# Two DeepNorm layers in split fp32: which sublayer makes which adaLN gate columns

## The chip, the cores and the metric

The kernel is one program on one core of a Trainium2 chip. The metric is the device time of one execution in microseconds. Engines are called PE (TensorE), PEld (its weight load), DVE (VectorE), ACT (ScalarE), POOL (GpSimd) and SP (SyncE, which here issues the large transfers).

## The reference

Two layers; each has three sublayers: an FFN (s = 0), a mixer (s = 1), an FFN (s = 2). Nine adaLN vectors per layer come from one condition vector `c`.

```
cond = silu(c)
for l in range(2):
    mod = (cond @ ada_w[l] + ada_b[l]).reshape(-1, 3, 3, 1024)   # [sublayer, (shift, scale, gate)]
    for s in range(3):
        u = x * (1 + mod[:, s, 1]) + mod[:, s, 0]
        h = mixer(u) if s == 1 else 0.5 * (silu(u @ w_g) * (u @ w_up)) @ w_out
        x = layer_norm(alpha * x + (1 + mod[:, s, 2]) * h, ln_g[l, s], ln_b[l, s])
```

`x` is 256 tokens by 1024, the FFN's hidden width 2816. The mixer is one projection of `u` for four kinds of attention and for four gates, four branch products, each times its sigmoid gate, summed, and an output product. Every number is fp32.

## The kernel before

**Weights.** Each weight tile of 128 x 1024 comes from HBM into a buffer `raw` (a pool of five, `RB`), with a transfer that SP issues (L256). ACT rounds it to `hi` (L259), DVE makes the rest `lo = raw - hi` (L264), and PE takes three passes of the exact parts (L283 to L285, or L287 to L289). `raw` is free once DVE has made `lo`; pairs `hi`, `lo` lie in pools of six. Loads are emitted with a priority (`HP`) that moves them ahead of other work.

**adaLN columns.** `ada_cols(l, s, v)` is a list of four steps. Each step loads two tiles of 128 x 1024 (L304, 512 KB, into the same five `raw` buffers and on the same queue of SP) and lets DVE reduce each against the condition vector (L305), which leaves one column of `shift`, `scale` or `gate`. A vector takes eight tiles. `ada_gate` transposes a finished gate, sends it through DRAM and spreads it over the rows (`G`).

**Who makes what.** `sub_steps(l, s, nxt)` gives every sublayer twelve steps: four for its own gate, eight for the shift and scale of the next sublayer; with some steps go the fetches of the LayerNorm's rows and `ada_gate` (before step 4). The last FFN has eight empty steps in place of a next sublayer. An FFN spreads its steps evenly over its 22 blocks (`hidden`, then `steps.pop`); the mixer runs one at every fourth tick from tick 6 on, a tick being half a pair of projection tiles or a quarter of a branch.

**Around them.** A block of an FFN ends in `post`: ACT's `th`, DVE's `th` (L525) and `h` (L527), which frees one of two PSUM banks `mm`, then `hh` and `hl`. The first two blocks after a boundary go through a transpose `hT` (L611) of an `h` (L609). A branch of the mixer is four products into two PSUM banks `tp`; DVE multiplies each with its gate (`tg`, L1063), which frees the bank. Before each boundary `next_mod` (L383 to L385), which has a high priority, needs the scale and shift of the next sublayer.

All engines run their own instructions in order. The order within an engine is set by the scheduler that builds the program, from the emission order and the priorities. The scheduler hands a freed `raw` buffer to the next transfer in SP's order.

Of the kernel before, what the change touches and what calls it, by code (L numbers as in the profile page):

```python
# [11 lines left out]
F32 = mybir.dt.float32  # L12
# [6 lines left out]
D = 1024  # L19
T = 256  # L20
# [13 lines left out]
# columns of mix_w_in  # L34
# [5 lines left out]
# pairs of 128-column tiles whose products come out transposed  # L40
# [7 lines left out]
# offsets in the constants  # L48
C_COS, C_SIN, C_END = 0, 256, 512
# offsets in the constants of sums  # L50
R_ONE, R_SUF, R_FOX = 0, 128, 256
R_END = 256 + 640
# offsets in the masks
C_MC, C_MT, C_MA = 0, 384, 768
M_END = 768 + 1152
# depths of buffers, priorities and places of the pieces of work among each other
# [51 lines left out]
def _consts():  # L108
    c = np.zeros((128, C_END), np.float32)
    i = np.arange(128)  # L110
    r = np.zeros((128, R_END), np.float32)
    r[:, R_ONE:R_ONE + 128] = 1.0
    r[:, R_SUF:R_SUF + 128] = (i[:, None] >= i[None, :])
    # minus sums of the first and of the second key tile, by columns (q0 k0, q1 k0, q1 k1)
    for o in (0, 128, 512):
        r[:, R_FOX + o:R_FOX + o + 128] = -(i[:, None] <= i[None, :]).astype(np.float32)
    r[:, R_FOX + 256:R_FOX + 384] = -1.0
    half = ROT // 2
    inv = np.float32(THETA) ** (-(np.arange(half, dtype=np.float32) * np.float32(2.0 / ROT)))
    ang = np.arange(T, dtype=np.float32)[:, None] * inv[None, :].astype(np.float32)  # L120
    cos, sin = np.cos(ang.astype(np.float64)).T, np.sin(ang.astype(np.float64)).T
    ct, st = np.ones((128, T)), np.zeros((128, T))
    for b in (0, 64):
        ct[b:b + 8], ct[b + 8:b + 16] = cos, cos
        st[b:b + 8], st[b + 8:b + 16] = sin, -sin
    c[:, C_COS:C_COS + 256], c[:, C_SIN:C_SIN + 256] = ct, st
    m = np.zeros((128, M_END), np.float32)
    q0, q1, k = i[:, None], i[:, None] + 128, np.arange(256)[None, :]
    bad = lambda ok: np.where(ok, 0.0, BIG)
    m[:, C_MC:C_MC + 128] = bad(k[:, :128] <= q0)  # L130
    m[:, C_MC + 128:C_MC + 384] = bad(k <= q1)
    m[:, C_MT:C_MT + 256] = -bad(i[:, None] < np.arange(256)[None, :])
    m[:, C_MT + 256:C_MT + 384] = -bad(i[:, None] < i[None, :])
    rules = [lambda d: (d >= 0) & (d <= 128), lambda d: (d >= 0) & (d % 4 == 0), lambda d: (d >= 0) & (d % 16 == 0)]
    for g, rule in enumerate(rules):
        m[:, C_MA + g * 128:C_MA + g * 128 + 128] = bad(rule(q0 - k[:, :128]))
        m[:, C_MA + 384 + g * 256:C_MA + 384 + g * 256 + 256] = bad(rule(q1 - k))
    return np.eye(128, dtype=np.float32), c, np.concatenate([m, r], axis=1).astype(ml_dtypes.bfloat16)
# [3 lines left out]
def trunk(ctx: ExitStack, tc: tile.TileContext, x, xT, crow, ada0, adac, adab, w_in0, w_in0x, gcol, bcol, ln_g, ln_b,  # L142
# [46 lines left out]
    # 2 silu(c) = c * (1 + tanh(c / 2))  # L189
# [43 lines left out]
    held = {"ins": [], "left": 0, "free": 0}  # L233

    def behind():
        """queue what follows behind the boundary that has just been emitted, on its engines."""
        stack = ExitStack()
        for i in held["ins"]:
            stack.enter_context(tc.issue_after(i))
        return stack  # L240
# [4 lines left out]
    def load(*srcs):  # L245
        """srcs: [128, n] each; the parts of their halves, which are loaded in turns."""
# [32 lines left out]
    def split_mm(ps, w, xh, xl, start, stop, w_stationary=True):  # L279
        """ps += w^T x by three passes of exact parts."""  # L280
# [11 lines left out]
    mods = {(l, s): {} for l in range(DEPTH) for s in range(3)}  # L292

    def ada_cols(l, s, v):
        """steps that leave sum_k cond_k W_kn + b_n (+ 1) in columns [128, n // 128]."""
        key = ("shift", "scale", "gate")[v]

        def run(c):
            if c == 0:
                mods[(l, s)][key] = ap_.tile([P, KT], F32, tag=key, bufs=2, name=key)  # L300
# [9 lines left out]
    def ada_gate(l, s):  # L310
        """steps that leave sum_k cond_k W_kn + b_n + 1 in every row of G."""
# [19 lines left out]
    def modulate(src, uh, ul, gd, bd, on_act):  # L331
        """parts of src * gd + bd; src may lie in PSUM."""
# [9 lines left out]
    def fetch_row(dst, row):  # L342
        """a row of DRAM into one partition of each 32; spread_row spreads it from there."""
# [16 lines left out]
    def sub_steps(l, s, nxt):  # L360
        """steps beside a sublayer's products: its gate and its LayerNorm's rows, the modulation of what follows."""
        st = mods[(l, s)]
        nx = ada_cols(*nxt, 0) + ada_cols(*nxt, 1) if nxt else [lambda: None for _ in range(8)]
# [11 lines left out]
        seq = ada_cols(l, s, 2) + nx  # L375
        return [both(*before.get(n, []), f) for n, f in enumerate(seq)]

# [10 lines left out]
    def boundary(rt, accs, i, G, g, b, u, nxt):  # L388
        """rows: r = ALPHA x + G O, then LayerNorm; into u: its modulation for what follows."""
# [78 lines left out]
        def finish(gate):  # L468
            """the second token tile, behind products of the first one in what follows."""
# [22 lines left out]
    # column groups of a sublayer's last products: (token tile, first column, columns)  # L492
    TAIL = ((0, 0, 512), (0, 512, 512), (1, 0, 512), (1, 512, 512))

# [1 line left out]
    def ffn(l, s, u, nxt, steps, first=False):  # L496
# [61 lines left out]
        if first:  # L558
            f0 = F0
            banks = [mm_bank() for _ in range(2)] + [acc_bank() for _ in range(4)] + [tp_bank() for _ in range(2)]  # L560
            for n in range(KT):
# [3 lines left out]
                for k in range(2 * F0):  # L565
                    # up to block N0 the last two banks hold the pair after the first F0
# [72 lines left out]
    def mixer(l, u, nxt, steps):  # L639
# [9 lines left out]
        # pieces of attention, which take their turns between those of the projections  # L649
# [51 lines left out]
        def vproj(srcs, width, piece, extra=0):  # L701
            """extra: leading columns, of wf and of the index keys."""
# [29 lines left out]
        # columns of V in pieces of 384: B 0, C 256, D 512, A 768  # L732
# [7 lines left out]
        def scores(pss, qs, ks, start=True):  # L740
            """of two heads in their halves of the rows: q-tile 0 by keys 0..127, q-tile 1 by keys 0..255."""
# [4 lines left out]
        def transposed(p0, p1):  # L746
            """[q, keys] blocks -> [keys, (k0 q0, k0 q1, k1 q1)]."""
# [8 lines left out]
        def pv(y, heads):  # L756
            """y[64 j.., :] = sum over (v of key tile 0, of key tile 1, transposed weights) of heads[j]."""
# [11 lines left out]
        def y_out(y, k, t=None):  # L769
            """parts of what a branch is fed with; t: of one token tile only."""  # L770
# [10 lines left out]
        def soft(s_out, parts):  # L781
            """softmax of negated scores; parts: per q-tile a list of (psum, mask, columns of s_out)."""
# [35 lines left out]
        def index_scores(h):  # L818
# [11 lines left out]
            if h == 3:  # L830
                # keys that may not be seen take the value that marks a taken key
# [36 lines left out]
        def a_scores(t):  # L868
            """q-tile t of both heads of the three groups."""
# [16 lines left out]
        def a_blocks(t):  # L886
            """(group, head, key tile), in the order in which their products are taken."""
# [37 lines left out]
        def c_logs():  # L925
            """the logarithms of C, and with them those of D's forget gates."""
# [14 lines left out]
        def c_sums(j):  # L941
            """of two heads: the sums, and with them the weights."""
# [34 lines left out]
        def plan():  # L977
            """what runs after which piece of the projections, in steps of half a pair."""
# [24 lines left out]
            for n in range(S0, S0 + 4 * len(steps), 4):  # L1003
                on(n, step)
# [20 lines left out]
        # gates and branch products  # L1025
# [92 lines left out]

    u = new_u()
    for l in range(DEPTH):  # L1120
        u = ffn(l, 0, u, (l, 1), sub_steps(l, 0, (l, 1)), first=l == 0)
        u = mixer(l, u, (l, 2), sub_steps(l, 1, (l, 2)))
        nxt = (l + 1, 0) if l + 1 < DEPTH else None
        u = ffn(l, 2, u, nxt, sub_steps(l, 2, nxt))
# [55 lines left out]
```

## Time and profile before

| | |
|---|---|
| time, median of 3 runs (lowest, highest) | 1333.25 us (1328.18, 1336.28) |
| profiled execution, first to last instruction | 1336.7 us |
| PE, PEld busy | 1279.5, 1185.8 us |
| DVE, ACT, POOL busy | 1045.9, 655.5, 193.0 us |
| TensorE clock granted, mean | 0.987 of 2.4 GHz |
| moved by DMA | 300.41 MB, mean 225 GB/s |

The runs' times and the profiled execution come from different executions; 1336.7 us is the profiled one's own time. A busy time is the union of the instructions of an engine. Matmuls overlap each other in it, so a small wait of PE doesn't show as idle. The boundaries between the six sublayers lie at about 207, 471, 671, 872 and 1134 us.

### The profile page before, as it was taken

What the parts mean: (1) busy time and instruction counts of PE and PEld (TensorE: products, weight loads), DVE (VectorE), ACT (ScalarE), POOL (GpSimd) and SP (SyncE); (2) the same over time, 40 slices, a digit from 0 to 9 for tenths busy, and PEclk for the clock granted to TensorE, in tenths of its full rate; (3) what the DMA queues carried; (4) which work ended last, traced back from release to release, by engine and by line L of the source; (5) the groups of instructions that cost most, each with busy time, mean ns of one, the idle gap of its engine ahead of it and who ended that gap; (6) DMA issues with size and microseconds to landing.
All of it is one profiled execution on the core that took longest, in us unless ns stands there. A gap on an engine that the chain in (4) does not pass through costs nothing.

```text
span 1336.7 us, 23420 instructions
## 1 busy us (share of the span) xinstructions
PE 1279.5 (96%) x9178; PEld 1185.8 (89%) x9178; DVE 1045.9 (78%) x1661; ACT 655.5 (49%) x1023; POOL 193.0 (14%) x190
## 2 busy tenths in 40 slices
PE   6999998999999999999989999989999999899997
PEld 6989987899989889998979998988999998899996
DVE  7787888999855898876698876698997658986565
ACT  4644355457754445534345434354567544454440
POOL 0130004305011040000040000052060110400000
PEclk9999999999999989999999999989999999999999
DMA  9888992767755539877439877437677554596540
GB/s 340 317 294 317 314 312 95 254 193 254 254 177 188 190 132 319 307 265 248 149 138 315 301 266 243 140 126 248 201 252 242 189 190 158 174 328 199 184 142 32
DMA packets 85846, 300.41 MB, mean 225 GB/s; under 512 B 10604, under 2 KB 12316, under 8 KB 85736
## 3 DMA queue, kind: packets, MB, share of 16 engines
q1 hardware_dynamic: 84392, 298.00, 65.7%
q8 instruction: 72, 1.18, 0.3%
q10 hardware_dynamic: 576, 0.60, 0.1%
q0 software_dynamic: 768, 0.32, 0.1%
q14 instruction: 38, 0.31, 0.1%
HBM read 297.81 MB, written 1.07 MB: 224 GB/s over the span
## 4 chain that ended last, share of the span: by engine, by line
PE 57%; DMA 17%; DVE 16%; issue 5%; ACT 4%; POOL 1%; SPq 0%; DVEq 0%; ACTq 0%; POOLq 0%
PE mm L283 12%; PE mm L284 11%; PE mm L285 11%; DMA raw<-in_w_in_dram 10%; DVE lo L264 6%; DMA raw<-in_adac_dram 6%; PE acc L289 5%; PE acc L287 5%; PE acc L288 5%; DVE raw L305 2%; ACT hi L259 2%; DVE rt L415 2%; PE tp L283 1%; PE tp L284 1%; PE tp L285 1%
## 5 line engine op out<-in xcount | busy, mean ns | idle before, releaser
L264 DVE TENSOR_TENSOR lo<-raw,hi 128x1024 fp32r<-128x1024 f32 (+2 forms) x421 | 509.6, 1223 | 178.9 <-ACT hi L259 176.1
L259 ACT CAST hi<-raw 128x1024 fp32r<-128x1024 f32 (+1 forms) x422 | 434.6, 1040 | 354.6 <-PE mm L284 133.9
L283 PE MATMUL mm<-uh,hi 128*128 128x256 f32 x2032 | 576.8, 284 | 6.4 <-DVE h L527 5.4
L284 PE MATMUL mm<-ul,hi 128*128 128x256 f32 x2032 | 573.2, 282 | 0.0
L285 PE MATMUL mm<-uh,lo 128*128 128x256 f32 x2032 | 572.5, 282 | 0.3 <-DVE lo L264 0.3
L283 PEld LDWEIGHTS mm<-uh,hi 128*128 128x128 f32 x2032 | 385.0, 190 | 13.9 <-issue 6.3
L284 PEld LDWEIGHTS mm<-ul,hi 128*128 128x128 f32 x2032 | 385.1, 190 | 1.4
L285 PEld LDWEIGHTS mm<-uh,lo 128*128 128x128 f32 x2032 | 385.0, 190 | 0.8 <-DVE lo L264 0.5
L305 DVE CUSTOM_DVE_ANT_0 raw<-raw,cond_row,adab 128x1024 f32<-128x1024 f32 x128 | 164.1, 1292 | 43.2 <-DMA raw<-in_adac_dram 43.0
L287 PE MATMUL acc<-hi,hh 128*128 128x512 f32 x352 | 140.6, 399 | 1.7 <-ACT hh L533 1.6
L288 PE MATMUL acc<-lo,hh 128*128 128x512 f32 x352 | 139.1, 395 | 0.0
L289 PE MATMUL acc<-hi,hl 128*128 128x512 f32 x352 | 138.3, 396 | 0.4 <-POOL hl L534 0.4
L289 PEld LDWEIGHTS acc<-hi,hl 128*128 128x128 f32 x352 | 66.0, 188 | 17.8 <-DVE hl L534 1.2
L533 ACT CAST hh<-h 128x256 fp32r<-128x256 f32 x82 | 33.2, 405 | 98.7 <-DVE h L527 96.9
L287 PEld LDWEIGHTS acc<-hi,hh 128*128 128x128 f32 x352 | 66.1, 188 | 17.0 <-ACT hh L533 3.3
L405 POOL TENSOR_TENSOR rstd<-rstd,nhalf 128x1 f32<-128x1 f32 x12 | 7.6, 633 | 494.7 <-DVE rstd L404 494.7
L288 PEld LDWEIGHTS acc<-lo,hh 128*128 128x128 f32 x352 | 66.1, 188 | 13.9
L1065 POOL TENSOR_TENSOR merged<-merged,tg 128x512 f32<-128x512 f32 x16 | 23.0, 1451 | 143.8 <-DVE tg L1063 97.1
L289 PE MATMUL acc<-hi,ul 128*128 128x256 f32 (+1 forms) x128 | 41.3, 323 | 2.2 <-DVE ul L434 2.2
L287 PE MATMUL acc<-hi,uh 128*128 128x256 f32 (+1 forms) x128 | 41.7, 326 | 0.0
L534 DVE TENSOR_TENSOR hl<-h,hh 128x256 fp32r<-128x256 f32 x74 | 31.1, 420 | 12.6 <-ACT hh L533 12.6
L288 PE MATMUL acc<-lo,uh 128*128 128x256 f32 (+1 forms) x128 | 40.5, 316 | 0.0
(242 smaller groups left out, 1583.8 us busy)
## 6 DMA issues: line engine op xcount, KB each, us to landing
raw<-in_w_in_dram SPq DMA_DIRECT2D x174, 512.0 KB, 5.6
raw<-in_adac_dram SPq DMA_DIRECT2D x128, 512.0 KB, 5.4
raw<-in_mpair_dram SPq DMA_DIRECT2D x104, 512.0 KB, 5.1
raw<-in_w_out_dram SPq DMA_DIRECT2D x88, 512.0 KB, 5.4
ada<-in_ada_dram SPq DMA_DIRECT2D x16, 512.0 KB, 6.7
raw<-in_mwo_dram SPq DMA_DIRECT2D x16, 512.0 KB, 4.1
raw<-in_mv_dram SPq DMA_DIRECT2D x16, 384.0 KB, 3.5
raw<-in_mbr_dram SPq DMA_DIRECT2D x12, 512.0 KB, 3.9
```

The source lines that it names most:

```text
L259: nc.scalar.copy(hi[:, :half], raw[:, :half])
L264: held["lo"] = nc.vector.tensor_sub(lo[:, :half], raw[:, :half], hi[:, :half].bitcast(F32)).ins
L283: nc.tensor.matmul(ps, lhsT=wh, rhs=xh, start=start, stop=False)
L284: nc.tensor.matmul(ps, lhsT=wh, rhs=xl, start=False, stop=False)
L285: nc.tensor.matmul(ps, lhsT=wl, rhs=xh, start=False, stop=stop)
L287: nc.tensor.matmul(ps, lhsT=xh, rhs=wh, start=start, stop=False)
L288: nc.tensor.matmul(ps, lhsT=xh, rhs=wl, start=False, stop=False)
L289: return nc.tensor.matmul(ps, lhsT=xl, rhs=wh, start=False, stop=stop).ins
L305: nc.vector.tensor_tensor_reduce(raw, raw, cond_row, 0.5, adab_sb[:, l * 3 + s, v, n:n + 1], ALU.mult, ALU.add, accum_out=t[:, n:n + 1])
L415: nc.vector.tensor_scalar(rt[:, t, hs], rt[:, t, hs], mv[t][:, 0:1], rstd[t], op0=ALU.subtract, op1=ALU.mult)
L533: nc.scalar.copy(hh, h)
L534: eng.tensor_sub(hl, h, hh.bitcast(F32))
```

## The change

The steps of each sublayer come from a plan, `ada_plan`. A mixer makes, after its own gate and the next FFN's shift and scale, that FFN's gate as well: 16 steps. The FFN behind the first mixer, (0,2), makes the shift and scale of the next layer's first FFN and half of that FFN's gate: 10 steps. That next FFN, (1,0), makes the other half and the shift and scale of its mixer: 10 steps. The last FFN, (1,2), makes none: its steps carry only the fetches, in 8 empty steps. The first FFN is as it was. In the mixer the first nine steps stand where they stood; the further ones come every 3 or 4 ticks in place of every 4. Gate columns get four buffers in place of two. Comments were taken out, which shifts line numbers by 10 to 12.

```diff
-                mods[(l, s)][key] = ap_.tile([P, KT], F32, tag=key, bufs=2, name=key)
+                mods[(l, s)][key] = ap_.tile([P, KT], F32, tag=key, bufs=4 if v == 2 else 2, name=key)
...
-    def sub_steps(l, s, nxt):
+    def ada_plan():
+
+        gate = {k: ada_cols(*k, 2) for k in mods}
+        mod = {k: ada_cols(*k, 0) + ada_cols(*k, 1) for k in mods}
+        work = {}
+        for l in range(DEPTH):
+            here, after, nxt = (l, 0), (l, 2), (l + 1, 0)
+            work[here] = (gate[here] if l == 0 else gate[here][2:]) + mod[(l, 1)]
+            work[(l, 1)] = gate[(l, 1)] + mod[after] + gate[after]
+            work[after] = mod[nxt] + gate[nxt][:2] if nxt in mods else []
+        return work
+
+    def sub_steps(l, s):
...
-        seq = ada_cols(l, s, 2) + nx
+        seq = list(ada[(l, s)])
+        seq += [lambda: None] * (GG + GD + 1 - len(seq))
...
-            for n in range(S0, S0 + 4 * len(steps), 4):
-                on(n, step)
+            for n in range(len(steps)):
+                on(S0 + 4 * min(n, 8) + 7 * max(0, n - 8) // 2, step)
...
+    ada = ada_plan()
```

The change moves instructions on DVE and SP. On DVE, in the second half of the (0,2) FFN, around the last two tiles of columns, before:

```order
L525 SCALAR_TENSOR_TENSOR th<-th,mm 128x256
L305 ISA raw,scale<-raw,cond_row,adab 128x1024
L305 ISA scale 128x1
L264 TENSOR_TENSOR lo<-raw,hi 128x1024
L383 TENSOR_TENSOR gd<-gcol,scale 128x8
L384 TENSOR_TENSOR bd<-bcol,scale 128x8
L527 SCALAR_TENSOR_TENSOR h<-th,mm 128x256
```

and after:

```order
L305 ISA raw,gate<-raw,cond_row,adab 128x1024
L305 ISA gate 128x1
L264 TENSOR_TENSOR lo<-raw,hi 128x1024
L537 SCALAR_TENSOR_TENSOR th<-th,mm 128x256
L539 SCALAR_TENSOR_TENSOR h<-th,mm 128x256
L264 TENSOR_TENSOR lo<-raw,hi 128x1024
L546 TENSOR_TENSOR hl<-h,hh 128x256
```

The last tile is a gate's, it stands ahead of `th`, and nothing stands between `th` and `h`.

On DVE, in the first mixer, ahead of the `tg` of the third branch (numbers tell buffers apart), before:

```order
L779 TENSOR_TENSOR y_4364<-acc_4552,y_4364 128x256
L264 TENSOR_TENSOR lo_4761<-raw_4758,hi_4760 128x1024
L264 TENSOR_TENSOR lo_4767<-raw_4764,hi_4766 128x1024
L264 TENSOR_TENSOR lo_4833<-raw_4830,hi_4832 128x1024
L264 TENSOR_TENSOR lo_4839<-raw_4836,hi_4838 128x1024
L264 TENSOR_TENSOR lo_4897<-raw_4894,hi_4896 128x1024
L264 TENSOR_TENSOR lo_4903<-raw_4900,hi_4902 128x1024
L1063 SCALAR_TENSOR_TENSOR tg_4559<-tg_4559,tp_4770 128x512
```

and after (the second half of it; ahead of it stand two more `lo` and the reduction of raw_4880):

```order
L305 ISA raw_4883,gate_4692<-raw_4883,cond_row_84,adab_89 128x1024
L305 ISA gate_4692 128x1
L264 TENSOR_TENSOR lo_4846<-raw_4843,hi_4845 128x1024
L264 TENSOR_TENSOR lo_4852<-raw_4849,hi_4851 128x1024
L305 ISA raw_4974,gate_4692<-raw_4974,cond_row_84,adab_89 128x1024
L305 ISA gate_4692 128x1
L305 ISA raw_4977,gate_4692<-raw_4977,cond_row_84,adab_89 128x1024
L305 ISA gate_4692 128x1
L264 TENSOR_TENSOR lo_4916<-raw_4913,hi_4915 128x1024
L264 TENSOR_TENSOR lo_4922<-raw_4919,hi_4921 128x1024
L1075 SCALAR_TENSOR_TENSOR tg_4565<-tg_4565,tp_4777 128x512
```

Four reductions of gate tiles now stand among the six `lo`, in two pairs, each pair with two `lo` behind it. SP's queue for the same place, after the change:

```order
L256 DMA raw_4771<-in_mbr_dram 128x1024
L304 DMA raw_4790<-in_adac_dram 128x1024
L304 DMA raw_4793<-in_adac_dram 128x1024
L256 DMA raw_4843<-in_mpair_dram 128x1024
L256 DMA raw_4849<-in_mpair_dram 128x1024
L304 DMA raw_4880<-in_adac_dram 128x1024
L304 DMA raw_4883<-in_adac_dram 128x1024
L256 DMA raw_4913<-in_mpair_dram 128x1024
L256 DMA raw_4919<-in_mpair_dram 128x1024
L304 DMA raw_4974<-in_adac_dram 128x1024
L304 DMA raw_4977<-in_adac_dram 128x1024
```

Before, no L304 stood between these projections' loads. DVE reads raw_4974 right after the two `lo` that follow its reading of raw_4883; SP can issue raw_4974 when raw_4883 has been read. The second mixer has the same order.

## Rows read from the trace of the kernel before

**Rows 1.** The page: span, busy time by engine, the column reductions and their transfers

```profile
span 1336.7 us, 23420 instructions
...
PE 1279.5 (96%) x9178; PEld 1185.8 (89%) x9178; DVE 1045.9 (78%) x1661; ACT 655.5 (49%) x1023; POOL 193.0 (14%) x190
...
L305 DVE CUSTOM_DVE_ANT_0 raw<-raw,cond_row,adab 128x1024 f32<-128x1024 f32 x128 | 164.1, 1292 | 43.2 <-DMA raw<-in_adac_dram 43.0
...
raw<-in_adac_dram SPq DMA_DIRECT2D x128, 512.0 KB, 5.4
```

**Rows 2.** Three stretches: PE, PEld, DVE, ACT, POOL busy (instructions), clock, DMA share, GB/s

```profile
495.40:670.20 174.80, 172.41 (x1184) 159.57 (x1185) 134.12 (x195) 79.74 (x112) 1.70 (x3) 0.99 0.75 257
695.30:871.20 175.90, 172.56 (x1184) 159.50 (x1185) 133.10 (x195) 78.40 (x112) 1.70 (x3) 0.99 0.74 252
1158.40:1328.00 169.60, 169.54 (x1176) 157.22 (x1176) 112.18 (x154) 72.75 (x99) 2.14 (x3) 1.00 0.57 191
```

**Rows 3.** PE's waits, 774 to 842 us; the first row also answers 574 to 641

```profile
PE mm L283 <- DVE h L527: 2.3, 1, 2.3
PE acc L287 <- ACT hh L533: 0.9, 1, 0.9
```

**Rows 4.** Slices of the mixers and the FFNs, columns as in rows 2

```profile
370.00:440.00 70.00, 67.83 (x559) 66.29 (x558) 39.39 (x50) 34.45 (x59) 11.90 (x8) 0.98 0.56 182
400.00:410.00 10.00, 10.00 (x87) 10.00 (x86) 4.34 (x4) 4.68 (x8) 0.00 (x0) 1.00 0.54 179
610.00:620.00 10.00, 8.60 (x54) 8.37 (x55) 7.21 (x13) 5.72 (x8) 0.00 (x0) 0.83 0.90 330
810.00:820.00 10.00, 7.66 (x51) 7.54 (x51) 7.92 (x15) 5.25 (x8) 0.00 (x0) 0.83 0.97 344
380.00:390.00 10.00, 7.83 (x55) 7.79 (x54) 8.01 (x19) 5.26 (x14) 5.95 (x4) 0.83 0.50 167
1040.00:1050.00 10.00, 8.70 (x73) 7.72 (x72) 7.70 (x21) 4.82 (x16) 3.17 (x3) 1.00 0.83 283
```

**Rows 5.** DVE's timeline in (0,2): start, duration, instruction [idle before, releaser]

```profile
604.62 1.28 DVE L305 CUSTOM_DVE_ANT_0 raw<-raw,cond_row,adab 128x1024 f32<-128x1024 f32 x1 [3.85 <-DMA raw<-in_adac_dram]
...
608.11 0.42 DVE L525 SCALAR_TENSOR_TENSOR th<-th,mm 128x256 f32<-128x256 f32 x1
608.44 1.28 DVE L305 CUSTOM_DVE_ANT_0 raw<-raw,cond_row,adab 128x1024 f32<-128x1024 f32 x1
...
610.93 0.42 DVE L527 SCALAR_TENSOR_TENSOR h<-th,mm 128x256 f32<-128x256 f32 x1
```

**Rows 6.** PE's waits, 370 to 440 us and 1035 to 1103 us

```profile
PE tp L283 <- DVE tg L1063: 2.2, 1, 2.2
...
PE tp L283 <- DVE tg L1063: 1.3, 1, 1.3
```

**Rows 7.** DVE's timeline in the first mixer, ahead of the second branch's `tg`

```profile
372.16 1.28 DVE L305 CUSTOM_DVE_ANT_0 raw<-raw,cond_row,adab 128x1024 f32<-128x1024 f32 x1 [4.71 <-DMA raw<-in_adac_dram]
...
373.38 2.35 DVE L264 TENSOR_TENSOR lo<-raw,hi 128x1024 fp32r<-128x1024 f32 x2
377.16 1.28 DVE L305 CUSTOM_DVE_ANT_0 raw<-raw,cond_row,adab 128x1024 f32<-128x1024 f32 x1 [1.43 <-DMA raw<-in_adac_dram]
...
381.48 0.68 DVE L1063 SCALAR_TENSOR_TENSOR tg<-tg,tp 128x512 f32<-128x512 f32 x1
```

**Rows 8.** SP's timeline: the issue of the tile that DVE reads at 377.16

```profile
373.48 0.33 SPq L304 DMA_DIRECT2D raw<-in_adac_dram  x1
```

**Rows 9.** DVE's timeline in the first mixer, around the third branch's `tg`

```profile
399.43 1.23 DVE L264 TENSOR_TENSOR lo<-raw,hi 128x1024 fp32r<-128x1024 f32 x1 [3.69 <-ACT hi L259]
...
413.35 1.45 DVE L1063 SCALAR_TENSOR_TENSOR tg<-tg,tp 128x512 f32<-128x512 f32 x2
415.83 0.69 DVE L1063 SCALAR_TENSOR_TENSOR tg<-tg,tp 128x512 f32<-128x512 f32 x1 [1.02 <-PE tp L285]
```

**Rows 10.** PE's waits, 1150 to 1180 us

```profile
PE hT L611 <- DVE h L609: 0.7, 1, 0.7
```

More of the change, by code (lines that the diff above doesn't have):

```diff
@@ L358, in both @@
         return run
-    def sub_steps(l, s, nxt):
+    def ada_plan():
[9 more added lines that the diff above has]
+    def sub_steps(l, s):
         st = mods[(l, s)]
-        nx = ada_cols(*nxt, 0) + ada_cols(*nxt, 1) if nxt else [lambda: None for _ in range(8)]
         def fetch(key, row):
@@ L1117, in first_block @@
         modulate(xT_sb[:, n], u[0][:, n], u[1][:, n], c0[:, n, 1:2], c0[:, n, 0:1], True)
+    ada = ada_plan()
     u = new_u()
     for l in range(DEPTH):
[L1121 to L1124, printed above, removed]
+        u = ffn(l, 0, u, (l, 1), sub_steps(l, 0), first=l == 0)
+        u = mixer(l, u, (l, 2), sub_steps(l, 1))
+        u = ffn(l, 2, u, (l + 1, 0) if l + 1 < DEPTH else None, sub_steps(l, 2))
 def _layout(x, c, ada_w, ada_b, ln_g, ln_b, ffn_w_in, ffn_w_out, mix_w_in, mix_b_gate, mix_b_forget, mix_w_branch, mix_w_out):
```

## The prediction

> **What bounds the kernel now.** I read the page first [rows 1]: TensorE (PE) is busy for 1279.5 of 1336.7 us. It is in nearly every stage the engine that the others serve, so a change that only moves VectorE (DVE) and DMA work can win no more than the places where PE stands still because of that work. A busy PE is counted with overlapping ends, so the second view is a comparison of equal work. In each of the last three FFNs I take the stretch from the hT transposes to the last product [rows 2]. The (0,2) and (1,0) FFNs run 1184 matmuls in 174.8 and 175.9 us; the (1,2) FFN runs the same ones, less eight boundary transposes, in 169.6 us. The first two make nearly all of their 24 column tiles in there, the last most of its 8. The 5.2 and 6.3 us are what the columns can cost an FFN.
>
> The third view, PE's waits, says where they are [rows 3]. Each of the two FFNs has one wait of 2.3 us of a first pass (L283) for `h` (L527), and (1,0) has 0.9 us more for `hh`. Right after, the granted clock of a 10 us slice is 0.83 [rows 4]: some of it ran at 1.2 GHz instead of 2.4, which lost (1 - 0.83) x 10 = 1.7 us. So 4.0 of 5.2 us and 4.9 of 6.3 us are named; the rest goes to the eight transposes and gaps too short to be listed.
>
> The fourth view, DVE's timeline, says why `h` was late [rows 5]. DVE works in order. It sat 3.85 us for a column tile, got to `th` at 608.11, and then did another L305 (608.44), a `lo` and the two small operations of `next_mod` before `h` at 610.93. The last scale column was pulled in between `th` and `h` because `next_mod` (high priority) needs it.
>
> In the mixers the same view shows one PE wait each, for `tg` (L1063) of 2.2 and 1.3 us [rows 6]; the first is followed by a clock of 0.83, the second by 1.00 [rows 4]. Here too DVE had waited for columns: 4.71 us, then 1.43 us, then `tg` at 381.48 [rows 7].
>
> **The change, part by part.** The number of column tiles stays 128, so DMA bytes and DVE work in total stay. The first FFN keeps its 12 steps. What moves is 4 tiles out of each middle FFN, 8 out of the last one, and 8 into each mixer.
>
> *Middle FFNs.* Each loses 4 transfers and 4 reductions of 1.29 us [rows 1], 5.2 us of DVE work that was hidden except at its end. There the order changes too: the scale columns come earlier, the last two steps are gate columns that no high-priority work asks for, and `h` follows `th` at once. Had `h` followed `th` at 608.44, it would have been done at 608.86, about when PE came for the bank. I therefore take back the whole named loss: 4.0 + 4.9 = 8.9 us. Bounds: 0 (DVE still waits for a gate tile just before a `th`, and the wait stays) and 5.2 + 6.3 = 11.5 us (all of it).
>
> *Last FFN.* Its first gate tile stood between `th` and `h` of the first block, and PE waited 0.7 us for that `h` [rows 10]. No tile is left there: -0.7 us (0 to -1.0). `ada_gate` finds its gate already made. The steps without work move the rows' fetches to later blocks, on GpSimd's queue, which idles there; still long before the boundary: 0.
>
> *Mixers.* Eight more transfers and reductions, all in the stretch with the gate projections: 8 x 1.29 = 10.3 us of DVE in 70 us of which it is busy for 39.4 [rows 4], so the work alone costs nothing. What costs is order. SP issues in order, into five raw buffers, which DVE frees in its order: a transfer starts when the fifth reading before it is done. If DVE reads a column tile soon after that, it stands still for the rest of the transfer, and everything behind it waits: `lo`, `y` and `tg`.
>
> There are two places. First, the `tg` of 381.48. Two scale reductions now come one pair of weight halves earlier, and one gate reduction that is issued only three readings before comes in front of `tg`. Walking the chain with the durations of the rows gives `tg` at about the same time; I take 0, with -2.2 - 1.7 (the wait and its clock fall go) and +2 for each mixer as bounds.
>
> Second, the four `tg` of the third branch, at 413.35 now [rows 9]. Before, only six `lo` (and `y`) stood ahead of them from 399.43 on. Afterwards the six `lo` have four gate reductions among them in two pairs. From 400.0 (one more reduction comes just before) the work is 6 x 1.17 + 4 x 1.22 = 11.9 us (two `lo` take 2.35 us, and the start after a reduction comes 1.22 later [rows 7]). Each pair is released by the reading two `lo` ahead of it, so DVE stands for Lat - 2.35 each time, Lat being the time from issue to landing, and, by estimate, 0.4 us more for the second tile of a pair. The first `tg` starts at 400.0 + 11.9 + 2 (Lat - 2.35) + 0.8 = 408.0 + 2 Lat. PE needs it at 413.7: its product for the third `tg` was ready at 415.83, is 12 matmuls long (1.4 us at 87 in 10 us [rows 4]), and needs the bank which the first `tg`, of 0.7 us, frees. So PE waits 2 Lat - 5.7 us. A transfer alone took from 373.48 to 377.16, 3.7 us [rows 7, 8]; the median of all column transfers is 5.4 us [rows 1], most of them in FFNs with the DMA busier. With two or three in flight I take 4.1, nearer to the lone one: 2.5 us. After waits of 2.2 and 2.3 us the clock fell, after 1.3 us it did not [rows 3, 4, 6]: I add 1.7. That is 4.2 us in each mixer, 8.4 us; with 3.7 us in place of 4.1, 1.7 us of wait; with 5.4, 5.1 us.
>
> The Trainium skill ("DMA: Bandwidth & Descriptors", Anatomy of one DMA) gives 2.0 us plus the bytes at 436 GB/s for one transfer on GpSimd's path, an estimate of 3.2 us for 512 KB. By that, the wait would be 0.7 us, without a fall of the clock, and the sum 7 us lower. The one lone transfer of this trace took longer (3.7 us), so the rows stand.
>
> **Sum**, against the profiled execution's 1336.7 us: -8.9 - 0.7 + 8.4 = -1.2, 1335.5 us. The runs' median is 1333.25, 3.4 us below the profiled one; from the median I forecast **1332 us**: no change. One per cent, 13 us, is about what a measurement of this kernel can tell from no change.
>
> **The rivals.**
> - *The mixers hide it all.* If transfers land in 3.7 us or less and PE's wait stays near the 1.3 us that left the clock alone, each mixer costs 0 to 1.7 us, and the FFNs' 9.6 us stay: 1324 to 1327, say 1325. For it: the DMA share is 0.56 there [rows 4]. Against: DVE waited 4.71 us for a tile in the same stage [rows 7].
> - *The mixers lose more than the FFNs win (slower).* The mechanism is the same queue of DVE in front of the third branch's `tg`. With Lat at 5.4 a mixer loses 5.1 + 1.7, and with the first `tg` late by another 1.0 it is 7.8: 1333.25 - 9.6 + 15.6 = 1339, up to 1346 if the FFNs give back only a third. It decides from 2 Lat - 5.7 + 1.7 = 4.8, that is Lat = 4.4 us, on.
> - *The FFNs don't get faster.* The tiles left at the end of a middle FFN are released only two readings ahead, as those of before were; DVE then still comes late to `th`. The gain is 0 to 2 us and the mixers' 8.4 remain: 1340.
>
> **How the numbers follow.** Forecast 0.5 (1328 to 1336), mixers hide it 0.27, mixers lose more 0.14, FFNs keep their waits 0.09. The range 1321 to 1343 holds the first, nearly all of the second (its end with 11.5 us from the FFNs is 1333.25 - 12.2 = 1321), and most of the other two. Faster by over 1% (below 1320) takes the FFNs' upper bound and a mixer gain together: 0.05. Slower by over 1% (above 1346.6) takes Lat above 5.4 and no gain in the FFNs: 0.06. The rest, 0.89, is within 1%.
>
> **What the profile after would show.** The stretches of rows 2 for the (0,2) and (1,0) FFNs at about 170.5 us, with no wait for `h` and a clock of 1.00 to their ends: the FFN term is right. A PE wait for `tg` of 2 to 3 us in each mixer, some 35 us after the first one, with DVE idle for column tiles before it: the mixer term is right; its absence makes the first rival, a wait of 5 us the second. The (1,2) FFN without a wait at hT. The prediction is wrong by more than its range if the eight tiles hold up `hi` and `lo` so long that PE waits for weights in the gate projections, which the trace of before shows nowhere.

## The result, and the profile after

The changed kernel takes 1357.58 us in the median of 5 runs (1350.64 to 1359.34), the kernel before 1333.25 (1328.18 to 1336.28): a ratio of 1.0168, interval 1.0141 to 1.0195. It is slower by 1.4 to 1.95%, and its time lies above the range of the prediction (1321 to 1343). The profiled execution after (1350.64 us) is the shortest of the five, and the one before, with a span of 1336.7 us, took longer than any of the timed ones (1336.28 us at most), so the two pages differ by only 12.0 us.

The page after, with the rows that answer to [rows 1] and the group of products that wait for `tg`:

```profile
span 1348.7 us, 23426 instructions
...
PE 1276.7 (95%) x9178; PEld 1182.0 (88%) x9178; DVE 1049.3 (78%) x1661; ACT 656.0 (49%) x1023; POOL 192.0 (14%) x190
...
L305 DVE CUSTOM_DVE_ANT_0 raw<-raw,cond_row,adab 128x1024 f32<-128x1024 f32 x128 | 166.5, 1310 | 54.3 <-DMA raw<-in_adac_dram 54.0
...
L283 PE MATMUL tp<-y,hi 128*128 128x256 f32 x112 | 37.0, 330 | 17.4 <-DVE tg L1075 17.4
...
raw<-in_adac_dram SPq DMA_DIRECT2D x128, 512.0 KB, 5.2
```

PE and DVE are as busy as before; the span has grown by idle time. Ahead of the 128 column reductions DVE now stands 54 us, where it stood 43. PE's waits say where that arrives (total in us, times, longest):

```profile
PE tp L283 <- DVE tg L1075: 17.4, 4, 5.1
PE hT L623 <- DVE h L621: 5.0, 4, 2.2
PE acc L289 <- DVE hl L546: 4.5, 3, 2.0
...
PE mm L283 <- DVE h L539: 1.2, 2, 0.6
```

The waits for `tg` were two, of 2.2 and 1.3 us [rows 6]; they are four: 5.1 and 4.2 us in the first mixer, 4.6 and 3.6 us in the second. The waits of the FFNs for `h` [rows 3] are nearly gone, but waits for `hl` (L546) stand in their place. Cut at the first boundary transpose of each sublayer, the difference to the trace of before is: first FFN -1.2, first mixer +9.8, FFN (0,2) -2.5, FFN (1,0) -3.5, second mixer +9.8, last FFN -0.4 us. In these traces all of the loss is in the mixers.

DVE's timeline in the first mixer, ahead of the `tg` of the second branch (as [rows 7]):

```profile
370.39 2.36 DVE L264 TENSOR_TENSOR lo<-raw,hi 128x1024 fp32r<-128x1024 f32 x2
378.72 1.28 DVE L305 CUSTOM_DVE_ANT_0 raw<-raw,cond_row,adab 128x1024 f32<-128x1024 f32 x1 [5.96 <-DMA raw<-in_adac_dram]
...
382.54 1.27 DVE L1075 SCALAR_TENSOR_TENSOR tg<-tg,tp 128x512 f32<-128x512 f32 x2
```

and ahead of that of the third (as [rows 9]):

```profile
399.66 1.28 DVE L305 CUSTOM_DVE_ANT_0 raw<-raw,cond_row,adab 128x1024 f32<-128x1024 f32 x1
...
407.52 1.28 DVE L305 CUSTOM_DVE_ANT_0 raw<-raw,cond_row,adab 128x1024 f32<-128x1024 f32 x1 [3.75 <-DMA raw<-in_adac_dram]
...
413.96 1.28 DVE L305 CUSTOM_DVE_ANT_0 raw<-raw,cond_row,adab 128x1024 f32<-128x1024 f32 x1 [1.62 <-DMA raw<-in_adac_dram]
...
416.04 1.29 DVE L305 CUSTOM_DVE_ANT_0 raw<-raw,cond_row,adab 128x1024 f32<-128x1024 f32 x1 [0.79 <-DMA raw<-in_adac_dram]
...
419.52 1.28 DVE L1075 SCALAR_TENSOR_TENSOR tg<-tg,tp 128x512 f32<-128x512 f32 x2
```

The issues of these tiles on SP:

```profile
372.78 7.59 SPq L304 DMA_DIRECT2D raw<-in_adac_dram  x2
...
400.97 1.76 SPq L304 DMA_DIRECT2D raw<-in_adac_dram  x2
...
410.10 1.47 SPq L304 DMA_DIRECT2D raw<-in_adac_dram  x2
```

From issue to reading the first of each pair took 5.9, 6.55 and 3.9 us, and DVE stood 0.8 us more for the second tile of the last pair. The first was issued at 372.78, when the pair of `lo` from 370.39 had just been done and had freed a buffer; DVE came to read it at once. The `tg` of the third branch is at 419.52, where it was at 413.35. Counted from the mixer's first boundary transpose, which came 1.2 us earlier in this trace, the `tg` of the second branch is 2.3 us later than before and that of the third 7.4 us; in the second mixer it is 2.8 and 8.9 us. The granted clock in the 10 us behind each of the four waits, first and second mixer (columns as in [rows 2]):

```profile
383.30:393.30 10.00, 10.00 (x66) 10.00 (x67) 8.44 (x17) 6.24 (x16) 5.95 (x4) 0.75 0.60 198
...
420.30:430.30 10.00, 10.00 (x63) 10.00 (x64) 5.25 (x5) 2.73 (x3) 5.94 (x4) 0.72 0.49 166
...
1052.00:1062.00 10.00, 9.98 (x65) 9.98 (x66) 8.50 (x17) 6.23 (x16) 5.93 (x4) 0.73 0.56 200
...
1088.50:1098.50 10.00, 10.00 (x73) 10.00 (x74) 6.05 (x6) 3.50 (x4) 5.95 (x4) 0.85 0.54 180
```

In these 10 us PE, always busy, does 63 to 73 products where it does 87 at full clock: by the clock, 2.5, 2.8, 2.7 and 1.5 us are lost behind the waits.

The stretches of the last three FFNs, cut as in [rows 2]:

```profile
503.70:676.30 172.60, 169.75 (x1184) 156.53 (x1185) 130.21 (x188) 79.53 (x112) 1.70 (x3) 1.00 0.72 249
701.30:873.90 172.60, 170.67 (x1184) 157.82 (x1185) 129.33 (x188) 79.73 (x112) 1.70 (x3) 0.99 0.72 244
1171.50:1340.10 168.60, 168.46 (x1177) 156.01 (x1177) 103.23 (x139) 70.50 (x97) 2.14 (x3) 1.00 0.51 168
```

172.6 us each, against 174.8 and 175.9 before and a forecast of 170.5. DVE's timeline in the middle of (0,2) shows the new wait:

```profile
588.87 0.40 DVE L539 SCALAR_TENSOR_TENSOR h<-th,mm 128x256 f32<-128x256 f32 x1
590.76 1.28 DVE L305 CUSTOM_DVE_ANT_0 raw<-raw,cond_row,adab 128x1024 f32<-128x1024 f32 x1 [1.49 <-DMA raw<-in_adac_dram]
...
591.97 2.36 DVE L264 TENSOR_TENSOR lo<-raw,hi 128x1024 fp32r<-128x1024 f32 x2
594.24 0.42 DVE L546 TENSOR_TENSOR hl<-h,hh 128x256 fp32r<-128x256 f32 x1
```

Behind the spreading of `G` (1.36 us on DVE) the block's `th` and `h` come late, a column tile and two `lo` stand between `h` and `hl`, and PE waits 2.0 us for that `hl`. (1,0) has the same order at the same place and waits 1.9 us. Before, the tile stood between `th` and `h` of a later block [rows 5].

### The profile page after: what moved, and what is told of

It is laid out like the page before. It is cut to its first block, busy times and chain, and to the rows that moved or that the text cites. A ratio compares the mean times of both kernels' runs of the same rounds, so it can differ in the third digit from the quotient of the medians.

```text
span 1348.7 us, 23426 instructions
## 1 busy us (share of the span) xinstructions
PE 1276.7 (95%) x9178; PEld 1182.0 (88%) x9178; DVE 1049.3 (78%) x1661; ACT 656.0 (49%) x1023; POOL 192.0 (14%) x190
## 4 chain that ended last, share of the span: by engine, by line
PE 57%; DVE 16%; DMA 16%; ACT 5%; issue 5%; POOL 1%; DVEq 0%; ACTq 0%; SPq 0%; POOLq 0%
PE mm L283 11%; PE mm L284 11%; PE mm L285 11%; DMA raw<-in_w_in_dram 8%; DVE lo L264 7%; DMA raw<-in_adac_dram 6%; PE acc L289 6%; PE acc L287 5%; PE acc L288 5%; ACT hi L259 3%; DVE raw L305 2%; DVE rt L427 2%; PE tp L283 1%; DVE ul L446 1%; PE tp L284 1%
## 5 line engine op out<-in xcount | busy, mean ns | idle before, releaser
L283 PE MATMUL tp<-y,hi 128*128 128x256 f32 x112 | 37.0, 330 | 17.4 <-DVE tg L1075 17.4
L318 POOL DMA_DIRECT2D gflat<-grow x6 | 3.4, 574 | 280.4 <-ACT grow L316 280.4
L283 PEld LDWEIGHTS tp<-y,hi 128*128 128x128 f32 x112 | 25.2, 225 | 20.4 <-DVE tg L1075 19.1
```

What stands on the lines that cost most here:

```text
L283: nc.tensor.matmul(ps, lhsT=wh, rhs=xh, start=start, stop=False)
```

## The experiments

Theory T: in the mixers DVE stands, in its order, for column tiles whose transfer starts only when DVE itself has freed a buffer one to three readings earlier; behind it the `tg` come late, PE stands, and its clock falls. Rivals: the added work, not the wait, delays `tg` (W); the number of tiles in the gate projections, not their place (P); the new order in the FFNs (F); chance (D). Each ratio is to the kernel before on the same chip (medians there 1334.7 to 1336.7 us). A difference in us beside a ratio is worked out from that ratio; the medians themselves give differences up to 2.1 us away from it.

### The changed kernel again

No edit; for a second trace.

> The changed kernel once more, for a second trace of it. Theory T: in the gate stage of each mixer DVE, in order, stands for column tiles whose transfers were released only one to three readings before, so the tg products of the second and the third branch come late, PE stands and its clock falls. By T the second trace has the four PE waits for tg again, 15 to 20 us in all, and each mixer about 10 us longer than before. Rival D: the loss differs from execution to execution and the waits of the first trace are chance; then the waits for tg come to under 10 us in this trace, or lie in other places. If this trace is some 7 us longer than the first one of the changed kernel, as the other executions were, the stage that is longer shows what the first trace left out.

Measured: 1353.32 us, ratio 1.0140 (1.0092 to 1.0188). The trace, of the longest execution, has a span of 1359.8 us.

```profile
PE tp L283 <- DVE tg L1075: 15.0, 4, 4.8
```

The four waits lie in the same places, the mixers are 8.6 and 11.0 us longer than in the trace of before; D falls. The 11 us between the two traces of this kernel lie mostly in the first FFN (4.7 us, a stage that the change leaves alone) and in the last (3.5). So a stage of one trace is known only to some 3 to 5 us, which holds for the comparison by sublayers in the section before too.

### The mixers' part alone

```diff
-            work[here] = (gate[here] if l == 0 else gate[here][2:]) + mod[(l, 1)]
-            work[(l, 1)] = gate[(l, 1)] + mod[after] + gate[after]
-            work[after] = mod[nxt] + gate[nxt][:2] if nxt in mods else []
+            work[here] = gate[here] + mod[(l, 1)]
+            work[(l, 1)] = gate[(l, 1)] + mod[after] + ada_cols(*after, 2)
+            work[after] = gate[after] + (mod[nxt] if nxt in mods else [lambda: None] * 8)
```

> The mixers as in the changed kernel, the FFNs as before: the eight gate tiles are made in the mixer and a second time in the FFN, so 16 tiles more are made than needed. Theory T: the whole loss is in the mixers and the FFNs win some, so this is slower than the changed kernel by what its FFNs won: 20 us over before in the profile (about 10 in each mixer), 1350 to 1362 us in the median, PE's waits for tg 15 to 20 us, its waits for h about 5 us as before. Rival F: the new order in the FFNs (the waits for hl) is what costs; then the mixers cost under 8 us together and the time is under 1342.

Measured: 1354.18 us, ratio 1.0124 (1.0085 to 1.0163), +16.6 us.

```profile
PE tp L283 <- DVE tg L1075: 16.9, 4, 4.7
PE mm L283 <- DVE h L539: 5.7, 3, 2.3
```

T's numbers; F falls. The mixers carry the loss. And these FFNs, in the order of before and with its waits for `h`, were 2.5 and 3.9 us shorter than in the trace of before, as much as those of the changed kernel: what the first comparison gave as the FFNs' win can be the spread of one trace.

### The FFNs' part alone

```diff
-            work[(l, 1)] = gate[(l, 1)] + mod[after] + gate[after]
+            work[(l, 1)] = gate[(l, 1)] + mod[after]
-                on(S0 + 4 * min(n, 8) + 7 * max(0, n - 8) // 2, step)
+                on(S0 + 4 * n, step)
-            nc.tensor.transpose(ps[:KT, :P], mods[(l, s)]["gate"], ident)
+            nc.tensor.transpose(ps[:KT, :P], mods[(l, min(s, 1))]["gate"], ident)
```

> The FFNs as in the changed kernel, the mixers as before: the next FFN's gate columns are left out (16 tiles), and that FFN takes the mixer's gate in their place. Theory T: the FFNs win 6 us: 1327 (1322 to 1331), PE's waits for tg as before (3.5 us), its waits for hl about 4.5 us as in the changed kernel. The prediction's FFN term alone, without waits for hl, would give 1323 to 1324. Rival F: the FFNs lose; 1340 or more.

Measured: 1337.15 us, ratio 1.0008 (0.9983 to 1.0033). No win is seen, where T expected 6 us and the prediction 9.6.

```profile
PE acc L289 <- DVE hl L546: 5.2, 2, 3.3
PE tp L283 <- DVE tg L1075: 3.3, 2, 2.2
```

The waits for `h` (5.4 us before, 0.7 us here) went, and those for `hl` came at about the same price. The two parts add up: +16.6 and +1.1 against +18.7 us for both.

### The reductions without the transfers, and the transfers without the reductions

```diff
+                moved = (s, v) == (2, 2)
-                nc.sync.dma_start(raw, adac[l, s, v, n])
+                if not moved:
+                    nc.sync.dma_start(raw, adac[l, s, v, n])
-                nc.vector.tensor_tensor_reduce(raw, raw, cond_row, 0.5, adab_sb[...],
+                nc.vector.tensor_tensor_reduce(raw, cond_row if moved else raw, cond_row, 0.5, adab_sb[...],
```

> The changed kernel with the eight extra tiles of each mixer not transferred: their reductions stay in DVE's queue at their full length, on a row that lies in SBUF (so these gate columns are other values). Theory T: what costs is DVE standing for transfers; PE's waits for tg fall from 17.4 us to under 6, and the time to 1323 to 1335. Rival W: the 10 us of extra DVE work in each gate stage is what makes tg late; then the waits for tg stay over 12 us and the time over 1343.

Measured: 1333.08 us, ratio 0.9970 (0.9946 to 0.9994). No wait for `tg` is left in the trace, not even those of before.

```profile
398.24 1.28 DVE L307 CUSTOM_DVE_ANT_0 raw<-cond_row,adab 128x1024 f32<-128x1024 f32 x1
```

The scheduler placed these reductions somewhat earlier; this is the last of the eight in the first mixer, and all stand ahead of the third branch's `tg`, which starts at 407.99. Without the transfers the work of the eight tiles costs nothing. The other half:

```diff
+                m = 8 if (s, v) == (2, 2) else 1024
-                nc.vector.tensor_tensor_reduce(raw, raw, cond_row, 0.5, ...
+                nc.vector.tensor_tensor_reduce(raw[:, :m], raw[:, :m], cond_row[:, :m], 0.5, ...
```

> The changed kernel with the eight extra tiles of each mixer transferred in full, but only 8 of their 1024 columns reduced (these gate columns are other values): the wait stays, 1.1 us of work goes for each tile. Theory T: DVE still stands for the transfers, so PE's waits for tg stay over half of the 15 to 17 us: 8 to 14 us, and the time 1342 to 1351. Rival W: it is the added work that makes tg late; under 6 us of waits and under 1340.

Measured: 1347.24 us, ratio 1.0089 (1.0058 to 1.0120). PE's waits for `tg` are 11.1 us. DVE at the first place:

```profile
382.89 0.23 DVE L306 CUSTOM_DVE_ANT_0 raw<-raw,cond_row,adab 128x8 f32<-128x8 f32 x1 [5.53 <-DMA raw<-in_adac_dram]
```

DVE stands 5.53 us for the tile of an instruction of 0.23 us; ahead of the third branch it stands 3.31, 1.03, 3.18 and 1.02 us. About two thirds of the loss (11.9 of 18.7 us) remain with nearly none of the work. So W falls as the main cause; the last third goes with the work, which lies in the same queue ahead of `tg`.

### The two places

`held["tg"]` is the last `tg` product that was emitted; a step between the brackets is queued behind it on DVE. First, six of the eight tiles behind the third branch:

```diff
-                on(S0 + 4 * min(n, 8) + 7 * max(0, n - 8) // 2, step)
+                on(S0 + 4 * min(n, 8) + 7 * max(0, n - 8) // 2 if n < 13 else 59 + 2 * (n - 13), step)
...
+                    with tc.issue_after(held["tg"]) if at["n"] > 58 else ExitStack():
+                        steps.pop(0)()
```

> The changed kernel, except that six of the eight extra gate tiles of each mixer stand behind the last tg product of the third branch; what stands ahead of the second branch's tg products (the first place) is as in the changed kernel. Theory T: each place costs by itself. The waits of about 5 us at the first place stay, those at the second go: PE waits 9 to 11 us for tg in all (two waits), each mixer is 4 to 6 us longer than before, the time 1342 to 1349 beside 1336.7 for before. Rival P: there is one disturbance, the number of extra tiles in the gate projections; then moving six of them changes little, 1350 or more, or the loss moves to the last branch.

Measured: 1346.87 us, ratio 1.0079 (1.0049 to 1.0108). The waits of the third branch are gone, those of the second are 3.3 and 2.8 us (5 us was expected), and 1.9 and 0.8 us are waited at the last branch. The third branch's `tg` is still 2.9 and 4.4 us later than before, counted from the mixer's start, against 7.4 and 8.9 us with both places: each place makes its own part of the delay. Then all eight behind the third branch, the first 12 steps where they stood before (`S0 + 4 * n if n < 12 else 59 + 2 * (n - 12)`):

> The changed kernel, except that the mixer's first 12 steps stand where they stood before and all eight extra gate tiles behind the last tg product of the third branch; the FFNs as in the changed kernel. Theory T: PE's waits for tg are as before, 3 to 4 us, and the time is that of the FFN change alone: 1333 to 1340 beside 1336.7. Rival P: eight more transfers and reductions cost wherever they stand in the gate projections; waits for tg or for lo over 8 us, 1345 or more.

Measured: 1345.03 us, ratio 1.0080 (1.0051 to 1.0110): T's 1333 to 1340 is missed. The waits of the second branch are those of before, the third has none, but PE now waits 2.9 and 4.3 us at the last branch.

```profile
440.89 2.49 DVE L265 TENSOR_TENSOR lo<-raw,hi 128x1024 fp32r<-128x1024 f32 x2 [0.84 <-ACT hi L260]
443.69 1.23 DVE L265 TENSOR_TENSOR lo<-raw,hi 128x1024 fp32r<-128x1024 f32 x1 [0.31 <-ACT hi L260]
444.83 0.68 DVE L1077 SCALAR_TENSOR_TENSOR tg<-tg,tp 128x512 f32<-128x512 f32 x1
```

DVE no longer stands for a tile here; the `lo` ahead of `tg` stand for `hi`. ACT's `hi` now stands for the weights' transfers (first row), where it stood for PE before (second row):

```profile
429.89 1.05 ACT L260 CAST hi<-raw 128x1024 fp32r<-128x1024 f32 x1 [5.21 <-DMA raw<-in_mpair_dram]
...
426.96 1.05 ACT L259 CAST hi<-raw 128x1024 fp32r<-128x1024 f32 x1 [2.47 <-PE mm L284]
```

The weights come late, and eight more transfers go through the same five buffers ahead of them. So P holds in part: this stretch had no room for all eight.

### The FFNs' waits priced

In the kernel before, the tile between `th` and `h` is moved one block on, behind an `hl`:

```diff
+            i_hl = eng.tensor_sub(hl, h, hh.bitcast(F32)).ins
+            if eng is nc.vector:
+                held.setdefault("hl", []).append(i_hl)
...
+                    with ExitStack() if first or ran != 11 else tc.issue_after(held["hl"][-4]):
+                        steps.pop(0)()
```

> The kernel before with one edit: in the two middle FFNs DVE takes the last two scale tiles behind the hl of the block in which they came, so no tile stands between th and h. This prices the prediction's FFN term by itself: it counted 4.0 + 4.9 us for PE's wait of 2.3 us for h, 0.9 for hh and the fall of the clock behind each. If a wait of that length is worth its whole named loss, PE's waits for h go from 5.4 to about 1 us and the time falls by 6 to 9 us, 1326 to 1331 beside about 1336. Rival N: the tile then delays the next block (another wait of the same length), or the loss is smaller than named; -2 to +2 us.

Measured: 1330.35 us, ratio 0.9961 (0.9936 to 0.9986), -5.2 us (-8.5 to -1.9); PE's waits for `h` go from 5.4 to 0.2 us. The win is real; 6 to 9 us were expected, and the named loss was 8.9. The same for the tile ahead of `hl` in the FFNs' part alone (step 8 in place of 11):

> The FFN change alone (mixers as before, eight gate tiles left out, the next FFN takes the mixer's gate) with one edit: of the FFNs' column tiles only the first step behind the spreading of G is queued behind an hl, one block later than it came; all others stay. In the kernel whose tiles all went behind hl, the held raw buffers starved the weights; here one pair is held for one block. Theory G: the two waits of 2.3 and 3.7 us for hl go and the time falls by 4 to 8 us under that of the FFN change alone, which was as before: 1328 to 1333 beside about 1336. Rival N: no change from before, 1334 to 1339. If even this holds up the weights: 1341 or more.

Measured: 1327.93 us, ratio 0.9930 (0.9905 to 0.9954), -9.4 us (-12.7 to -6.1; by the medians -7.8). The waits for `hl` are 0.5 us. So the FFNs' part of the change is worth about the 9.6 us of the prediction, once no tile stands ahead of `h` or `hl`. An attempt that queued every tile behind the `hl` of the block just emitted (`tc.issue_after` of the last one, all steps) was expected to do this:

> The FFN change alone, as above (mixers as before, eight gate tiles left out, the next FFN takes the mixer's gate), with one edit: in the last three FFNs DVE takes the column tiles of a step only behind the hl of the block that was just computed, so no tile stands between th, h and hl. Theory G: the FFN change won nothing in the median because the tiles went from a place ahead of h to one ahead of hl; with both free PE's waits for h and hl come to under 2 us together and the time to 1327 to 1333, 4 to 10 us under before. Rival N: these waits cost no more than they seem, or the wait goes on to th; the time stays at 1334 to 1340.

Measured: 1378.34 us, ratio 1.0322 (1.0286 to 1.0358); G is missed by 45 us.

```profile
PE mm L285 <- DVE lo L264: 7.0, 10, 0.8
```

PE waits for weights in many blocks. ACT's waits for the transfers of `w_in` in (0,2), in this run and before:

```profile
ACT hi L259 <- DMA raw<-in_w_in_dram: 53.6, 36, 5.7
...
ACT hi L259 <- DMA raw<-in_w_in_dram: 36.2, 24, 6.7
```

With the readings held back and the issues on SP left as they were, a tile of (0,2) keeps its buffer for 22.6 us in the median, from issue to the end of its reading, where it is 7.2 us in the FFN change alone; the weights get fewer buffers. The two middle FFNs are 19.6 and 18.0 us longer than in the trace of before. With the mixers' tiles late as well:

> The whole change with both mends: the eight extra gate tiles of a mixer behind the third branch's tg products, its first 12 steps where they stood before, and the FFNs' tiles behind hl. Theories T and G: waits for tg as before, for h and hl under 2 us, 1327 to 1334, under both kernels. If T alone holds, 1333 to 1340. Rival P: 1345 or more.

Measured: 1384.01 us, ratio 1.0377 (1.0323 to 1.0431): the same loss.

### A sixth raw buffer

`RB, QB = 6, 13` in place of `5, 15`, nothing else.

> The changed kernel with six raw buffers in place of five (the ring of small tiles goes from 15 to 13 to make room). Theory T: each transfer is released one reading earlier, about 1.2 us, and up to 2.4 where a lo pair stands between; PE's four waits for tg of 15 to 17 us fall to 6 to 12 us and the time to 1341 to 1349 beside about 1336 for before. Rival Q: SP's queue or the DMA's rate sets the landing, not the buffer; waits stay over 13 us, 1351 or more.

Measured: 1355.08 us, ratio 1.0140 (1.0105 to 1.0175), no better than with five.

```profile
PE tp L283 <- DVE merged L1073: 10.3, 2, 5.4
PE tp L283 <- DVE tg L1075: 8.7, 4, 4.3
...
347.53 1.28 DVE L305 CUSTOM_DVE_ANT_0 raw<-raw,cond_row,adab 128x1024 f32<-128x1024 f32 x1 [5.29 <-DMA raw<-in_adac_dram]
```

The wait for the second branch shrank, but the planned order put a tile ahead of the first branch's `merged` (the DVE row), and PE waits there, 10.3 us in the two mixers. The smaller ring of small tiles was not tried by itself.

### All of the change, with its tiles in other places

The mixer's first 12 steps stand where they stood before, one step of the new ones behind the second branch's `tg`, three behind the third's; in the FFNs step 8 is held as above.

```diff
+PLACES = (6, 10, 14, 18, 22, 26, 30, 34, 38, 42, 46, 50, 51, 59, 61, 64)
+PINS = (12, 13, 14, 15)
...
-                on(S0 + 4 * min(n, 8) + 7 * max(0, n - 8) // 2, step)
+                on(PLACES[n], step)
...
+                    with tc.issue_after(held["tg"]) if len(PLACES) - len(steps) in PINS else ExitStack():
+                        steps.pop(0)()
```

> The whole change, nothing left out, with its tiles in other places: in each mixer the first 12 steps stand where they stood before, two of the eight extra gate tiles behind the last tg product of the second branch and six behind that of the third; in the middle FFNs the one step behind the spreading of G is queued behind an hl, as in the run that did this to the FFN change alone. Theory T with G: place, not number, is what costs: PE's waits for tg 3 to 7 us, no wait for hl over 1 us, and the time is the FFN's win of 9 us less at most 4 in the mixers: 1326 to 1333 beside about 1336 for before, under both kernels. Rival P: eight more tiles in the gate projections cost wherever they stand; 1338 or more.

Measured: 1327.36 us, ratio 0.9930 (0.9902 to 0.9957): 9.3 us under the kernel before by the ratio (7.3 by the medians), and faster than both kernels. PE's waits for `tg`, and the stretches of the two middle FFNs, 169.6 and 168.6 us where they were 174.8 and 175.9:

```profile
PE tp L285 <- DVE tg L1081: 4.8, 4, 1.5
```

```profile
495.70:665.30 169.60, 169.27 (x1184) 156.76 (x1185) 130.46 (x187) 80.02 (x113) 1.70 (x3) 1.00 0.74 253
690.40:859.00 168.60, 168.53 (x1182) 156.44 (x1183) 128.78 (x187) 78.97 (x111) 1.70 (x3) 1.00 0.73 251
```

SP issues the first tile behind the third branch, and DVE reads it, like this:

```profile
406.41 4.52 SPq L306 DMA_DIRECT2D raw<-in_adac_dram  x2
...
415.87 0.69 DVE L1081 SCALAR_TENSOR_TENSOR tg<-tg,tp 128x512 f32<-128x512 f32 x1 [0.82 <-PE tp L287]
416.47 1.28 DVE L307 CUSTOM_DVE_ANT_0 raw<-raw,cond_row,adab 128x1024 f32<-128x1024 f32 x1
```

No wait stands before it: the tile was issued 10 us before DVE came to it, and in that time DVE did its `lo` and the four `tg` and stood for `hi` and for PE's products, which it must do anyway. The mixers are 0.1 and 1.7 us longer than in the trace of before, which is within the spread of a stage. So P holds only for eight in one stretch. That a few tiles held back do not starve the weights here, as they did in the FFNs, fits the trace of before: from 388 to 440 us ACT's `hi` stands for PE alone, and in the FFN (0,2) for transfers, 49.8 us in all. With six buffers and the same places:

> The kernel with the tiles in other places, and six raw buffers in place of five (ring of small tiles 13 in place of 15). With six buffers the planned order of DVE put the changed kernel's tiles still further ahead, and PE waited at the first branch in place of the second. Here the extra tiles are held in place. Theory O: the order was what undid the sixth buffer; with the order held it wins 3 to 8 us over five buffers, 1320 to 1328. Rival Q: the tiles land no earlier with a sixth buffer, or the first 12 steps, which are not held, go ahead again and make PE wait at the first branch; 1329 or more.

Measured: 1342.82 us, ratio 1.0051 (1.0028 to 1.0074). This is Q's outcome: the first 12 steps, which are not held, went ahead again.

```profile
PE tp L285 <- DVE merged L1079: 10.5, 2, 5.4
```

## Why the prediction was wrong

The sum of -1.2 us had three terms. Two of them failed, by about the same amount: the middle FFNs by some 10 us, the mixers by 8.

**Middle FFNs, -8.9.** The step that failed is "I therefore take back the whole named loss". `h` did follow `th` at once, and the loss behind it was real: with no tile ahead of `h` or `hl` the FFN change gives -9.4 us. But the tiles that stay went to the next place of the same kind, between `h` and `hl`, behind the spreading of `G`. The FFN change by itself gave +1.1 us (-2.3 to +4.4). The third rival ("the FFNs keep their waits") had named this outcome, with the waits at `th`.

**Last FFN, -0.7.** Not won: PE's waits for `h` at hT from 1150 to 1180 us were one of 0.7 us [rows 10] and are

```profile
PE hT L623 <- DVE h L621: 2.9, 2, 2.2
```

In the trace a `lo` stands between `th` and `h` in place of the tile. The size of this is inside the spread of a stage.

**Mixers, +8.4.** They cost 16.6 us. The mechanism at the third branch was right, and so was its formula: 408.0 plus the two measured times of 6.55 and 3.9 us gives 418.4, and the `tg` came at 419.52; the chain began at 400.9, where the last reduction ahead of it ended, and not at 400.0. Two steps failed.

One is the size of Lat, taken as 4.1 us, "nearer to the lone one"; the mean of the two here is 5.2. The transfer taken as lone [rows 8] was not: SP issued a weight tile at 374.62, before it landed. And the trace of before had longer ones in the same stage. The tile read at 372.16 [rows 7] is the first of the two issued from 364.74 on, 7.4 us earlier, and the last row gives the other column tiles issued from 340 to 390 us:

```profile
364.74 9.07 SPq L304 DMA_DIRECT2D raw<-in_adac_dram  x2
...
374.62 5.83 SPq L256 DMA_DIRECT2D raw<-in_mpair_dram  x4
...
DMA to landing us min/median/max: 4.4/5.9/6.9
```

At the third branch the wait in the first mixer is 4.2 us where 2.5 was forecast, and the clock behind it costs 2.8 in place of 1.7; in the second mixer it is 3.6 and 1.5.

The other is the first place, taken as 0: "`tg` at about the same time". Counted from the mixer's start the `tg` came 2.3 and 2.8 us later; PE's waits there grew from 2.2 and 1.3 us to 5.1 and 4.6, and what the clock loses behind them from 1.7 and 0 to 2.5 and 2.7 us. DVE stood 5.96 us for the gate tile ahead of it, the longest of the waits shown. The prediction has that tile issued "three readings before", and gives no sum for this place. The trace shows it issued at 372.78, when the reading just ahead of it in DVE's order had ended (370.39 and 2.36 us), so DVE stood for the whole transfer; the second mixer and the second trace of this kernel have the same. The run with six tiles moved, which leaves it as it is, stays 10.6 us over the kernel before; some of that is in the waits of 1.9 and 0.8 us at the last branch.

The sign that the prediction gave for a miss, PE waiting for weights in the gate projections, did not come: PE's waits after list none there. The second rival (the mixers lose more, 1339 to 1346) came nearest, and 1357.58 us lies above it too. It had the mechanism and the turning point (Lat over 4.4), but one place in each mixer in place of two, and a win in the FFNs that was not there.

## What to carry to other kernels

A prefetch that an in-order engine must read is priced by what stands behind it in that engine's queue: put it directly behind a place where the engine waits for others anyway, with its transfer issued early enough to land by then, and here it cost nothing that could be measured; where the engine came to it soon after its issue, the engine stood up to 5.96 us for it, and what was queued behind came late. A wait that is removed is only won if the work that made it finds a better place; look where it goes next before the loss is taken back. A sixth buffer did not help where the planner answered by moving the reading forward; whether it helps with the whole order held was not run.

## What was not expected of the hardware

A transfer of 512 KB took 3.9 to 6.55 us from issue to reading in the gate projections, and 3.7 us for the one of [rows 8], with the DMA engines only 0.56 busy over that stage [rows 4]: the share of busy time told nothing of what one transfer takes. The Trainium skill ("DMA: Bandwidth & Descriptors", Anatomy of one DMA) leads to an estimate of 3.2 us for one transfer on GpSimd's path; none of those four, which SP issued, was that short. Behind waits of 3.6 to 5.1 us the clock lost 1.5 to 2.8 us more; the kernel with its tiles in other places, with no wait for `tg` over 1.5 us, had a clock of 1.00 behind both places in the first mixer.
